# Gates behind the last mixer head, rho by Ln and Exp, and a tail laid out by token halves

## The chip, the cores and the metric

The kernel runs on one core of one Trainium2 chip. The metric is the device time of one execution in microseconds (us). A core has a matrix engine (TensorE, PE in the profile, with its weight loads as PEld), a vector engine (DVE), a scalar engine (ACT), a general engine (POOL), and a queue engine (SP) that here only issues transfers. Each works through its own instructions in order and waits for the others by semaphores. Transfers can be issued from SP and from POOL; sixteen DMA engines carry them out.

## The reference

One layer of a decoder trunk on 528 tokens (16 meta tokens, then 512), width 2048, and a final norm. Cut to what is computed:

```python
u = rmsnorm(h, norm1_g)                       # h: 528 x 2048
v_pool, v_lru, v_gelu, g_pool, g_lru = split(u @ w_in)
pool_out = per_group((window_mean(v_pool) - v_pool) @ pool_w) * pool_scale
xc = causal_conv4(v_lru)
r, i = sigmoid(xc @ gate_a + ab), sigmoid(xc @ gate_x + xb)   # per head of 256
a = exp(-8 * r * softplus(-lam))
state[t] = a[t] * state[t-1] + sqrt(1 - a**2)[t] * (i * xc)[t]
lru_out = state * gelu(v_gelu)
merged = sigmoid(g_pool) * pool_out + sigmoid(g_lru) * lru_out
h = h + merged @ w_out
h = h + relu(rmsnorm(h, norm2_g) @ w1)**2 @ w2
out = rmsnorm(h, final_g)[16:]
```

Channels lie on partitions, tokens in the free dimension.

## The kernel before

Every product is a sum of three: both operands are split into a rounded part (hi) and the rest (lo), and hi x hi, hi x lo and lo x hi add up in one PSUM bank. A class of its own, W (L45 to L161), brings the weights in chunks of 128 x 1024: SP issues the loads (L103), DVE adds raw chunks where a block form needs sums of them (L124), ACT makes the hi part (`whi`, L132), DVE the lo part (`wlo`, L133). Four raw buffers and four hi and lo buffers rotate; W.advance() prepares up to two splits ahead of the one in use, W.ready(n) goes on to split n.

The program runs through these stages.

1. Mixers, to about 480 us of the profile: a list of jobs written out by hand (L255 to L257). VL makes a channel block of the recurrence's input, VP one of the pooling input with its window sums on POOL (L542), GA the gates of a head (PE L363 into `ga`, sigmoids L496, and then the whole LRU: exponentials L506 to L508, the Sqrt L515, DVE steps, and a scan L524 whose result goes to DRAM, L525), PW the linear map of a pooling group (PE L358 into `ps_pw`, ACT copies `po` L564, a transfer L565). The list ends with VP_15, GA_7, PW_3.
2. Gates, from about 480 us: eight blocks each of three column ranges of w_in (gl, ge, gp), each block by seven products in place of eight (x11, t1, t2, ... of Strassen's kind; function strassen, L622). gl0 is the first. Its first product in bank A is copied by ACT to p1 (L642), another to u2 (L664), one of bank B to q5 (L646); DVE adds the banks to these (L742).
3. w_out with the residual, the row sums of squares and the second norm. finish_h (L809) writes a pair of row blocks of h to DRAM; middle (L948) is run after the first block of w1's products and makes rho, a factor per token, from PE's sum over partitions `ps_r`.
4. w1 with squared ReLU in 32 blocks, spilled to DRAM, and 5. w2 in groups, added into h by accumulating transfers.
6. The tail (L1103 to L1178): the last contributions to h for 16 row blocks m, first for token half 0, then for half 1; each is added into `acc` (L1157), squared (L1160), and the squares are added on POOL (L1164). norm_out (L1111) sums them over partitions on PE (L1114), and makes the factor r by Ln and Exp with one correcting step on DVE (L1117 to L1124); scale_out (L1130) applies it and issues the output's transfers on SP (L1139).

The order on each engine is set by a scheduler in the framework that places instructions by estimated costs when they become ready, within the order that data, buffers and explicit ties demand: `tc.issue_after(x)` places what is issued in it behind x, and a manual dependency does the same for a pair. One such tie, W.behind, is set in the last head's LRU: it holds DVE's weight sums of the first gates' splits that are prepared after that behind the last scan. Buffers of one name rotate; where a pool closes, the next pool in the same place waits for what still uses it.

## Time and profile before

| what | us |
|---|---|
| median of three runs (lowest, highest) | 2408.87 (2406.92, 2414.11) |
| the profiled execution | 2410.42 |
| its span, first to last instruction | 2408.6 |
| PE busy in it | 2362.7 |
| DVE busy | 1926.1 |
| ACT busy | 1211.2 |
| POOL busy | 310.0 |

The span is the core's time from the first to the last instruction; 1.8 us lie around it. Times in the rows are counted from its start. Busy shares are averages over stages with different limits, so the stages of the change are read on PE's timeline. A row of a timeline has the start, the length, the engine, the line, the operation with its output and inputs, and in brackets how long the engine stood idle before it and what ended that. An `x8` means that eight like instructions in a row are put in one.

### The profile page before, as it was taken

The page shows a single profiled execution, that of the slowest core. Times are in us where ns is not written, and L with a number is a line of the kernel's source. Part 1 is how long each engine was busy: PE and PEld are TensorE (multiplying, and loading weights), DVE is VectorE, ACT ScalarE, POOL GpSimd, SP SyncE. Part 2 cuts the span into 40 slices and gives each one's busy share as a digit, 9 for nine tenths or more (in the row PEclk, how much of TensorE's full clock was granted, in tenths as well). Part 3 has the DMA queues.
Part 4 walks back from the last instruction along what each step waited for, and adds up shares of the span by engine and source line. Part 5 has one row for each costly group of instructions (what it writes and reads, how often), then busy time and mean ns, then how long its engine had stood idle before and what let it go on. Part 6 is the DMA issues. An engine that isn't in the chain of part 4 may idle for free. (4 is left out here: it accounts for less than half of the span.)

```text
span 2408.6 us, 46240 instructions
## 1 busy us (share of the span) xinstructions
PE 2362.7 (98%) x19252; PEld 2313.6 (96%) x19252; DVE 1926.1 (80%) x2359; ACT 1211.2 (50%) x1631; POOL 310.0 (13%) x428
## 2 busy tenths in 40 slices
PE   8999999999999999999999999999989999999997
PEld 8999999999999999888999999999989999999997
DVE  7867766578888886378989888888879888888877
ACT  6654554445555554244445444444455555555544
POOL 0224343300000000022000000000100000000013
PEclk9999999999999999999999999999989999999998
DMA  5255555744444447568544545544576666666653
GB/s 196 88 167 175 173 169 183 259 171 141 149 141 149 157 151 266 166 214 279 163 156 152 160 152 164 166 161 156 186 202 172 178 179 193 187 189 184 169 183 105
DMA packets 119890, 418.73 MB, mean 174 GB/s; under 512 B 13888, under 2 KB 25280, under 8 KB 118016
## 3 DMA queue, kind: packets, MB, share of 16 engines
q1 hardware_dynamic: 78224, 251.82, 32.8%
q0 software_dynamic: 41312, 163.86, 21.3%
q8 instruction: 150, 2.46, 0.4%
q14 instruction: 60, 0.49, 0.1%
q10 hardware_dynamic: 144, 0.10, 0.0%
HBM read 324.89 MB, written 90.31 MB: 172 GB/s over the span
## 5 line engine op out<-in xcount | busy, mean ns | idle before, releaser
L133 DVE TENSOR_TENSOR wlo<-raw,whi 128x1024 fp32r<-128x1024 f32 (+2 forms) x388 | 467.6, 1207 | 127.4 <-ACT whi L132 127.1
L132 ACT ACTIVATE whi<-raw 128x1024 fp32r<-128x1024 f32 (+2 forms) x388 | 399.2, 1034 | 336.7 <-issue 88.1
L132 ACT ACTIVATE whi<-sum 128x1024 fp32r<-128x1024 f32 (+3 forms) x267 | 278.9, 1044 | 465.3 <-DVE sum L124 240.7
L133 DVE TENSOR_TENSOR wlo<-sum,whi 128x1024 fp32r<-128x1024 f32 (+3 forms) x267 | 320.7, 1201 | 80.7 <-ACT whi L132 76.4
L363 PE MATMUL ps_A<-a,whi 128*128 128x256 f32 x2048 | 359.0, 279 | 1.8 <-ACT whi L132 1.6
L363 PE MATMUL ps_Ab<-a,whi 128*128 128x256 f32 x1728 | 310.9, 280 | 3.5 <-DVE a L1002 1.7
L363 PEld LDWEIGHTS ps_A<-a,whi 128*128 128x128 f32 x2048 | 311.1, 189 | 2.9 <-ACT whi L132 1.8
L363 PE MATMUL ps_A<-a,wlo 128*128 128x256 f32 x1024 | 285.0, 278 | 0.0
L363 PEld LDWEIGHTS ps_Ab<-a,whi 128*128 128x128 f32 x1728 | 264.7, 190 | 4.1 <-DVE a L1002 1.9
L363 PE MATMUL ps_Ab<-a,wlo 128*128 128x256 f32 x864 | 242.0, 280 | 0.0
L124 DVE TENSOR_TENSOR sum<-sum,raw 128x1024 f32<-128x1024 f32 (+4 forms) x178 | 213.7, 1201 | 5.4
L363 PEld LDWEIGHTS ps_A<-a,wlo 128*128 128x128 f32 x1024 | 193.4, 189 | 0.0
L363 PE MATMUL ps_B<-a,whi 128*128 128x256 f32 x1024 | 177.8, 277 | 0.0
L363 PEld LDWEIGHTS ps_Ab<-a,wlo 128*128 128x128 f32 x864 | 164.6, 190 | 0.0
L363 PE MATMUL ps_vl<-a,whi 128*128 128x272 f32 (+1 forms) x896 | 163.3, 285 | 0.0
L363 PE MATMUL ps_vp<-a,whi 128*128 128x256 f32 (+1 forms) x896 | 162.8, 284 | 0.0
L363 PE MATMUL ps_wo<-a,whi 128*128 128x512 f32 x512 | 158.3, 390 | 0.0
L363 PEld LDWEIGHTS ps_B<-a,whi 128*128 128x128 f32 x1024 | 154.3, 188 | 0.1
L363 PE MATMUL ps_Bb<-a,whi 128*128 128x256 f32 x864 | 153.8, 278 | 0.0
L363 PE MATMUL ps_B<-a,wlo 128*128 128x256 f32 x512 | 141.9, 277 | 0.8 <-DVE wlo L133 0.8
L124 DVE TENSOR_TENSOR sum<-w,raw 128x1024 f32<-128x1024 f32 (+3 forms) x89 | 106.5, 1197 | 41.9 <-DMA raw<-w 37.8
L363 PEld LDWEIGHTS ps_vl<-a,whi 128*128 128x128 f32 x896 | 138.3, 189 | 0.3
(330 smaller groups left out, 5863.4 us busy)
## 6 DMA issues: line engine op xcount, KB each, us to landing
raw<-w SPq DMA_DIRECT2D x168, 512.0 KB, 4.3
raw<-w_in SPq DMA_DIRECT2D x135, 512.0 KB, 3.7
w<-w SPq DMA_DIRECT2D x56, 512.0 KB, 4.2
a<-ysp POOLq DMA_DIRECT2D x27, 896.0 KB, 6.3
hsp<-e POOLq DMA_DIRECT2D x33, 512.0 KB, 6.0
ysp<-t POOLq DMA_DIRECT2D x31, 512.0 KB, 5.0
w<-w_in SPq DMA_DIRECT2D x24, 512.0 KB, 3.8
ysp<-y POOLq DMA_DIRECT2D x31, 384.0 KB, 5.1
```

The lines of the kernel that those rows point to most:

```text
L124: nc.vector.tensor_tensor(self.raw[o], self.raw[x], self.raw[y], op=ALU.add)
L132: nc.scalar.activation(hi[:, s], raw[:, s], AF.Copy)
L133: nc.vector.tensor_tensor(lo[:, s], raw[:, s], hi[:, s].bitcast(F32), op=ALU.subtract)
L363: PE.matmul(o, a, b, start=first and i == 0, stop=last and i == 2, skip_group_check=True)
```

## The change

It has three parts and some moves that go with them.

**Mixers to gates.** The last head's sigmoids are no longer behind the first weight splits of the gates: W.hold ties the first one (whi80) behind the last sigmoid. The LRU of that head becomes a function of its own that is run behind PW_3, with W.ready to the second and fourth split of the first block before and between. The last group's pooling results get buffers from the ring in which the inputs of the recurrence are kept (`keep`, four buffers, two of them still held by the last head's), and their transfers and the last head's go on SP's queue instead of POOL's. For gl0, p1 and u2 lie in the buffer `scale`, which is not in use then, instead of the blocks' own pool; a manual tie puts the copy to p1 behind the first Sqrt, and the advance of the weights behind that copy.

**Rho.** pre_scale also makes v2 = s2 * s2 / D and loads the table of Ln and Exp, a load that stood at the tail. In middle, rho comes from Ln and Exp with one correcting step, in place of Sqrt, RECIPROCAL and one correcting step.

**Tail.** `acc` is laid out by pair, token half and row block, so that an output transfer has 2 KB in a row on each side instead of twice 1 KB, with the output tensor shaped to match and put in order on the host. The first norm's sums on PE come behind m = 3 of the second half and its factor behind m = 5 (both were behind m = 2). In the second half one square fewer is added on POOL; it goes to PE alone. finish_h writes h in the new layout, two transfers for one, and put_plain's results for w2 are laid out in the same way.

```diff
@@ Weights._split
-            nc.scalar.activation(hi[:, s], raw[:, s], AF.Copy)
+            with self.hold(i) if self.hold else contextlib.nullcontext():
+                nc.scalar.activation(hi[:, s], raw[:, s], AF.Copy)
@@ before the jobs
+        for i in range(2):
+            keep(f"turn{i}")
@@ job_GA
-                    S.activation(s, tokens(t), AF.Sigmoid,
+                    opened = S.activation(s, tokens(t), AF.Sigmoid,
...
+            if hd == HEADS - 1:
+                W.hold = lambda i: (tc.issue_after(opened.ins) if i == W.first_set
+                                    else contextlib.nullcontext())
+                W.ready(W.first_set + 2)
             W.advance()
+            if hd == HEADS - 1:
+                rest.append(lambda: lru(hd, pt))
+            else:
+                lru(hd, pt)
+        def lru(hd, pt):
...
-                S.activation(r, r, AF.Sqrt)
+                root = S.activation(r, r, AF.Sqrt)
+                if hd == HEADS - 1 and co == 0:
+                    W.root = root
...
-                G.dma_start(lr_sp[c % 8][:, c // 8, :], x[:, META:])
+                queue = nc.sync if hd == HEADS - 1 else G
+                queue.dma_start(lr_sp[c % 8][:, c // 8, :], x[:, META:])
@@ job_PW
-                z = tmp(f"po{c}")[:, :SEQ]
+                z = (keep if g == 3 else tmp)(f"po{c}")[:, :SEQ]
                 S.activation(z, t, AF.Copy, scale=pv("ps", c))
-                G.dma_start(pl_sp[c % 8][:, c // 8, :], z)
+                queue = nc.sync if g == 3 else G
+                queue.dma_start(pl_sp[c % 8][:, c // 8, :], z)
+            if rest:
+                W.ready(W.first_set + 4)
+                rest.pop()()
@@ strassen
+        if name == "gl0":
+            p1, u2 = scale[:, :HS], scale[:, HS:SEQ]
...
-                S.activation(p1, A, AF.Copy)
+                done = S.activation(p1, A, AF.Copy)
+                if name == "gl0":
+                    tc.add_manual_dep(W.root.ins, done.ins.name, ...
...
-                after(r)
-                W.advance()
+                done = after(r)
+                with tc.issue_after(done.ins) if name == "gl0" and r == "x11" else contextlib.nullcontext():
+                    W.advance()
@@ put_plain
-        n = 2 * int(c[0]) + int(c[1]) - 3
+        n = a + 2 * b if by_half else 2 * a + b
@@ finish_h
-        G.dma_start(h_sp[p].rearrange("p (a s) -> p a s", a=2), h)
+        for b in range(2):
+            dst = h_sp[p][:, b * SEQ : (b + 1) * SEQ].rearrange("p (a s) -> p a s", a=2)
+            G.dma_start(dst, h[:, :, b * HS : (b + 1) * HS])
@@ pre_scale
         S.activation(v2, s2, AF.Sqrt)
+        tc.keep_in_program_order(S.preload_act_table_set("natural_log_exp_and_others"))
         V.reciprocal(s2, v2)
+        V.scalar_tensor_tensor(v2, s2, 1.0 / D, s2, op0=ALU.mult, op1=ALU.mult)
@@ middle
+        V.scalar_tensor_tensor(rho, t, EPS * D, v2, op0=ALU.add, op1=ALU.mult)
...
-            V.tensor_scalar(a, t, 1.0 / D, EPS, op0=ALU.mult, op1=ALU.add)
-            for _ in range(2):
-                V.tensor_tensor(a, a, s2, op=ALU.mult)
-            S.activation(b, a, AF.Sqrt)
-            V.reciprocal(rho, b)
-            V.tensor_tensor(b, rho, rho, op=ALU.mult)
-            V.scalar_tensor_tensor(b, b, -0.5, a, op0=ALU.mult, op1=ALU.mult)
-            V.scalar_tensor_tensor(rho, b, 1.5, rho, op0=ALU.add, op1=ALU.mult)
+            S.activation(b, rho, AF.Ln)
+            S.activation(a, b, AF.Exp, scale=-0.5)
+            V.tensor_tensor(b, a, a, op=ALU.mult)
+            V.scalar_tensor_tensor(b, b, -0.5, rho, op0=ALU.mult, op1=ALU.mult)
+            V.scalar_tensor_tensor(rho, b, 1.5, a, op0=ALU.add, op1=ALU.mult)
@@ tail
-            ht = hp.tile([P, KD, SEQ], F32, name="acc")
+            ht = hp.tile([P, KD // 2, 2, 2, HS], F32, name="acc")
...
-    def norm_out(i, xs):
+    def total(i, xs):
         t = ps.tile([P, 512], F32, tag="ps", name=f"ps_n3_{i}")[:, :HS]
         for k, x in enumerate(xs):
             PE.matmul(t, ones, x, start=k == 0, stop=k == len(xs) - 1, skip_group_check=True)
+        return t
+
+    def root(i, t):
...
-            dst = out_d[m - 1 : m + 1, :, i * HS : (i + 1) * HS].rearrange("m p s -> p m s")
-            nc.sync.dma_start(dst, ht[:, m - 1 : m + 1, c])
-
-    tc.keep_in_program_order(S.preload_act_table_set("natural_log_exp_and_others"))
+            nc.sync.dma_start(out_d[m // 2, i], ht[:, m // 2, i].rearrange("p a s -> p (a s)"))
...
-            elif m < KD - 2:
+            elif m < KD - 2 - i:
                 G.tensor_tensor(sums[m % 2], sums[m % 2], q, op=ALU.add)
...
-            if i == 1 and m == 2:
-                r = norm_out(0, pend)
+            if i == 1 and m == 3:
+                pend = total(0, pend)
+            if i == 1 and m == 5:
+                r = root(0, pend)
...
-    r = norm_out(1, pend)
+    r = root(1, total(1, pend))
```

What moves on the engines stands in the order of their instructions (line, operation, output and inputs with buffer numbers; `whi80` is the hi part of weight split 80, the first of gl0, `gs700` the first sigmoid of the last head, `ga700` its bank, `a2` the input of the last pooling product, `po12` to `po15` the last group's results). First ACT from the mixers to the gates, before:

```order
L132 ACTIVATE whi79_5404<-raw79_5151 128x1024
L132 ACTIVATE whi80_5465<-raw80_5205 128x1024
L132 ACTIVATE whi81_5513<-sum80_5511 128x1024
L496 ACT_TABLE_LOAD
L496 ACTIVATE gs700_5357<-ga700_5344,par_71 128x528
L548 ACTIVATE a2_897<-pd15_5333 128x512
...
L564 ACTIVATE po12_5449<-ps_pw12_5436,par_71 128x512
...
L564 ACTIVATE po14_5495<-ps_pw14_5482,par_71 128x512
...
L132 ACTIVATE whi82_5569<-sum80_5511 128x1024
L132 ACTIVATE whi83_5598<-raw83_5473 128x1024
...
L642 ACTIVATE p1_gl0_5540<-ps_Agl0_5537 128x256
...
L664 ACTIVATE u2_gl0_5541<-ps_Agl0_5537 128x256
```

And in the change, where `scale_80` with 256 columns is first p1, then u2:

```order
L134 ACTIVATE whi79_5406<-raw79_5153 128x1024
L500 ACT_TABLE_LOAD
L500 ACTIVATE gs700_5359<-ga700_5346,par_71 128x528
L565 ACTIVATE a2_899<-pd15_5335 128x512
...
L134 ACTIVATE whi80_5410<-raw80_5207 128x1024
L134 ACTIVATE whi81_5420<-sum80_5418 128x1024
...
L581 ACTIVATE po14_5475<-ps_pw14_5462,par_71 128x512
...
L134 ACTIVATE whi83_5499<-raw83_5424 128x1024
...
L529 ACT_TABLE_LOAD
...
L667 ACTIVATE scale_80<-ps_Agl0_5548 128x256
...
L134 ACTIVATE whi84_5628<-w2181_5414 128x1024
...
L695 ACTIVATE scale_80<-ps_Agl0_5548 128x256
```

The sigmoids stand ahead of whi80, po14 and whi83 ahead of the last Sqrt, p1 behind it, and whi84 to whi87, which stood ahead of p1 or u2, behind p1. On SP's queue in the same place, where before nothing stood between the loads:

```order
L104 DMA w2185_5428<-w_in 128x1024
L583 DMA pl4_167<-po12_5443 128x512
...
L583 DMA pl7_170<-po15_5491 128x512
L542 DMA lr7_162<-xc15_5212 128x512
L104 DMA raw86_5632<-w_in 128x1024
L104 DMA raw87_5664<-w_in 128x1024
```

Four pl transfers and lr7, the last channel's, stand ahead of the loads raw86 and raw87.

Then DVE at rho (`scale_80` is s2 and later rho; `r2a` and `r2b` are work buffers), before:

```order
L958 TENSOR_SCALAR r2a_12532<-ps_r_12522 128x512
...
L960 TENSOR_TENSOR r2a_12532<-r2a_12532,scale_80 128x512
...
L960 TENSOR_TENSOR r2a_12532<-r2a_12532,scale_80 128x512
...
L962 RECIPROCAL scale_80<-r2b_12533 128x512
...
L963 TENSOR_TENSOR r2b_12533<-scale_80 128x512
...
L964 SCALAR_TENSOR_TENSOR r2b_12533<-r2b_12533,r2a_12532 128x512
L133 TENSOR_TENSOR wlo291_12581<-raw216_12243,whi291_12580 128x1024
L965 SCALAR_TENSOR_TENSOR scale_80<-r2b_12533,scale_80 128x512
L124 TENSOR_TENSOR sum216_12609<-w21217_12245,raw218_12464 128x1024
```

and in the change:

```order
L989 SCALAR_TENSOR_TENSOR scale_80<-ps_r_12532,v2_11055 128x512
L135 TENSOR_TENSOR wlo289_12503<-sum212_12348,whi289_12502 128x1024
...
L997 TENSOR_TENSOR r2b_12544<-r2a_12543 128x512
...
L998 SCALAR_TENSOR_TENSOR r2b_12544<-r2b_12544,scale_80 128x512
L135 TENSOR_TENSOR wlo291_12589<-raw216_12251,whi291_12588 128x1024
L999 SCALAR_TENSOR_TENSOR scale_80<-r2b_12544,r2a_12543 128x512
...
L125 TENSOR_TENSOR sum216_12617<-w21217_12253,raw218_12474 128x1024
```

Three of the steps and the RECIPROCAL are gone, and the weight sums and the lo parts of splits move up by as much.

Last DVE in the tail, where half 1 goes on and the first norm's factor `r3_0` is made, before:

```order
L1157 TENSOR_TENSOR acc_26763<-ps_w2l_1_2_27354,acc_26763 128x256
L1119 TENSOR_SCALAR r3_0_27370<-ps_n3_0_27365 128x256
...
L1124 SCALAR_TENSOR_TENSOR ps_r3_0_27376<-r3_0_27370 128x256
L1136 SCALAR_TENSOR_TENSOR acc_26763<-acc_26763,par_71,ps_r3_0_27376 128x256
L1157 TENSOR_TENSOR acc_26763<-ps_w2l_1_3_27378,acc_26763 128x256
L1136 SCALAR_TENSOR_TENSOR acc_26763<-acc_26763,par_71,ps_r3_0_27376 128x256
L1157 TENSOR_TENSOR acc_26763<-ps_w2l_1_4_27389,acc_26763 128x256
```

and in the change:

```order
L1191 TENSOR_TENSOR acc_26771<-ps_w2l_1_3_27372,acc_26771 128x256
L1156 TENSOR_SCALAR r3_0_27412<-ps_n3_0_27383 128x256
L1191 TENSOR_TENSOR acc_26771<-ps_w2l_1_4_27388,acc_26771 128x256
...
L1161 SCALAR_TENSOR_TENSOR ps_r3_0_27418<-r3_0_27412 128x256
L1172 SCALAR_TENSOR_TENSOR acc_26771<-acc_26771,par_71,ps_r3_0_27418 128x256
L1191 TENSOR_TENSOR acc_26771<-ps_w2l_1_6_27420,acc_26771 128x256
L1172 SCALAR_TENSOR_TENSOR acc_26771<-acc_26771,par_71,ps_r3_0_27418 128x256
```

The factor's steps stand between the additions into `acc` (L1157 before, L1191 in the change) instead of in one row, three row blocks later.

More of the change, by code (lines that the diff above doesn't have):

```diff
@@ L59, in __init__ @@
         self.behind = lambda i: contextlib.nullcontext()
+        self.hold = None
     def chunk(self, src):
@@ L641, in after @@
             if r == "x11":
-                S.activation(p1, A, AF.Copy)
+                done = S.activation(p1, A, AF.Copy)
+                if name == "gl0":
+                    tc.add_manual_dep(W.root.ins, done.ins.name,
+                                      mybir.DependencyInfo(mybir.DependencyClass.NoSync, mybir.DependencyReason.DATA),
+                                      reason="order")
+                return done
             elif r == "x21":
@@ L692, in strassen_pair @@
         A, B, C = ([bank(x, name) for name in names] for x in "ABC")
-        puts = [put_plain(e) for e in es]
+        puts = [put_plain(e, True) for e in es]
         spare = {"p1": scale[:, :HS], "u2": scale[:, HS:SEQ], "q5": es[1][:, 3 * HS :]}
@@ L1155, in build @@
                 W.advance()
-            h = ht[:, m, c]
+            h = ht[:, m // 2, i, m % 2]
             V.tensor_tensor(h, t, h, op=ALU.add)
@@ L1221 @@
     h = np.empty((KD, P, SEQ), np.float32)
-    for i in range(KD):
-        h[ORDER[i // 2] + 8 * (i % 2)] = got[i]
+    for q in range(KD // 2):
+        for a in range(2):
+            for b in range(2):
+                h[ORDER[q] + 8 * a, :, b * HS : (b + 1) * HS] = got[q, b, :, a * HS : (a + 1) * HS]
     return c(h.reshape(D, SEQ).T).reshape(1, SEQ, D)
```

19 lines of the change are left out of this document (11 added, 8 removed).

## The prediction

> **What bounds the kernel now.** I read the page first: engines, then the slices of the clock.
>
> ```profile
> span 2408.6 us, 46240 instructions
> PE 2362.7 (98%) x19252; PEld 2313.6 (96%) x19252; DVE 1926.1 (80%) x2359; ACT 1211.2 (50%) x1631; POOL 310.0 (13%) x428
> PEclk9999999999999999999999999999989999999998
> ```
>
> TensorE (PE) is busy 98% at nearly full clock, and no part of the change removes a matmul; so it can only win idle time, half clock, and the end behind the last product. The waits of PE, with sum, count and longest, say where idle time is:
>
> ```profile
> PE ps_Agl L363 <- ACT p_gl L642: 3.5, 1, 3.5
> PE ps_pw L358 <- ACT gs L496: 3.1, 1, 3.1
> ```
>
> Both, the largest that the change touches, lie in the passage from mixers to gates. Then I read PE's timeline at these places and at the end (start, length, instruction, idle before with what ended it).
>
> **Part 1, mixers to gates.** PE's rows are the first pooling product, the first and the resuming gl0 product, and gl0's last; then three stretches (length, busy time of PE, PEld, DVE, ACT, POOL, clock, DMA share, GB/s).
>
> ```profile
> 466.75 0.73 PE L358 MATMUL ps_pw<-a,whi 128*128 128x512 f32 x2 [3.09 <-ACT gs L496]
> 479.60 0.40 PE L363 MATMUL ps_Agl<-a,whi 128*128 128x256 f32 x2
> 486.94 0.39 PE L363 MATMUL ps_Cgl<-a,wlo 128*128 128x256 f32 x1 [0.95 <-DVE wlo L133]
> 493.30 0.80 PE L363 MATMUL ps_Agl<-a,whi 128*128 128x256 f32 x2 [3.49 <-ACT p_gl L642]
> 507.08 0.28 PE L363 MATMUL ps_Agl<-a,wlo 128*128 128x256 f32 x1
> ...
> 468.20:471.60 3.40, 3.40 (x10) 2.68 (x9) 0.35 (x1) 3.37 (x6) 2.51 (x2) 0.55 1.00 396
> 493.20:498.60 5.40, 5.30 (x25) 5.30 (x26) 4.92 (x5) 0.33 (x2) 0.54 (x1) 0.50 0.81 310
> 498.60:502.00 3.40, 3.40 (x29) 3.25 (x29) 1.23 (x1) 1.33 (x2) 0.00 (x0) 1.00 0.49 154
> ```
>
> The last stretch prices a 256-column matmul at full clock: 3.40 / 29 = 0.117. The pooling products (48 of 512 columns, twice that each by estimate) are 11.3, gl0 (7 x 24) 19.7, together 31.0. From 463.66 (466.75 less 3.09) to 507.36 are 43.7 us, so 12.7 are lost: 7.5 idle (3.09 + 0.95 + 3.49), the rest nearly all half clock, one window of 3.4 us behind each long idle time, some 1.7 us each, with the second longer.
>
> ACT around the first idle time, ACT's copy that ends the second, and DVE's last scan:
>
> ```profile
> 463.63 1.06 ACT L132 ACTIVATE whi<-sum 128x1024 fp32r<-128x1024 f32 x1 [4.80 <-PE ga L363]
> 464.70 1.28 ACT L496 ACT_TABLE_LOAD   x1
> 466.00 0.70 ACT L496 ACTIVATE gs<-ga,par 128x528 f32<-128x528 f32 x1
> 467.19 0.63 ACT L548 ACTIVATE a<-pd 128x512 fp32r<-128x512 f32 x1 [0.49 <-DVE pd L545]
> 492.87 0.38 ACT L642 ACTIVATE p_gl<-ps_Agl 128x256 f32<-128x256 f32 x1 [1.61 <-DMA lr<-xc]
> 481.02 1.26 DVE L524 TENSOR_TENSOR_SCAN xc<-n,gs 128x528 f32<-128x528 f32 x1
> ```
>
> The weight split stood, waiting 4.80 us, ahead of the sigmoid for which the pooling product's bank waits; the change puts the sigmoids first. So 3.09 goes. What is late next is the last pooled block: its hi split is at 467.19 behind a DVE result whose POOL sums do not move by more than a microsecond, and the products reach it earlier than now. I take back 1.5. The window then holds less idle than today's, its half clock goes too (+1.7): 3.09 - 1.5 + 1.7 = 3.3, and gl0 starts near 476.3.
>
> gl0 today takes 27.8 us for 19.7 of work, so 8.1 lost. The copy at 492.87 waited for the buffer of a result's transfer; in the change p1 and u2 lie in another place and this wait is gone. New is that ACT reaches p1 only behind the Sqrt, and that behind the fourth block result, po14, whose buffer po12's transfer must have left. That transfer, now on SP's queue, is issued near 473 while the DMA engines are full. Its price is the row of a weight load in such a time:
>
> ```profile
> raw<-w_in SPq DMA_DIRECT2D x1, 512.0 KB, 10.7
> 454.00:456.00 2.00, 2.00 (x19) 2.00 (x18) 1.43 (x2) 0.00 (x0) 0.00 (x0) 1.00 1.10 459
> ```
>
> The transfer is half as large and today's rush ends near 480, so it lands at 477 to 480. From there the rows behind it on ACT (po14 0.69, e1 0.63, whi83 1.06, po15 0.69, load 1.28, Sqrt 0.70) put p1's start between PE's need, 476.3 + 48 x 0.117 = 481.9, and 484.8: idle 0 to 2.9. Behind p1 stand the splits that today come before it: whi84 and its lo part, among the last head's DVE steps; the third product waits 2.3 to 3.2 for them. With no or two half-clock windows (0 to 3.4) gl0 loses 3.1 to 8.5: against 8.1 a gain of 5.0 to a loss of 0.4, and with the 3.3 the whole is 2.9 to 8.3. I take 5: nearer the low end, since ACT and DVE are in order here and nothing of the last head's work has gone. On SP the loads raw86 and raw87 now stand behind four pl transfers and lr7, which waits for the last scan (482.3 today); at 0.33 an issue that costs nothing while the scan ends before some 490.
>
> The Trainium skill, "DMA: Bandwidth & Descriptors", section "Queues, rings and completion order", says that a DMA engine takes packets from its queues in turn. By that the small transfer would not wait for the fills ahead of it, p1 would be at 482 and the gain 8. The 10.7 us of a load issued amid such fills speak against it.
>
> **Part 2, rho.** PE first, then DVE, with ACT's root:
>
> ```profile
> 1134.67 1.13 PE L952 MATMUL ps_r<-ssq,ones 128*128 128x512 f32 x2 [2.42 <-DVE ssq L820]
> 1144.89 0.50 PE L363 MATMUL ps_A<-a,whi 128*128 128x256 f32 x2 [0.21 <-DVE y L1025]
> 1151.72 0.39 PE L363 MATMUL ps_B<-a,wlo 128*128 128x256 f32 x1 [0.76 <-DVE wlo L133]
> 1156.16 0.51 PE L363 MATMUL ps_A<-a,whi 128*128 128x256 f32 x2 [1.57 <-ACT whi L132]
> 1157.11 0.62 PE L363 MATMUL ps_C<-a,whi 128*128 128x256 f32 x2 [0.44 <-ACT whi L132]
> ...
> 1136.80 0.69 DVE L958 TENSOR_SCALAR r2a<-ps_r 128x512 f32<-128x512 f32 x1
> 1141.21 3.35 DVE L962 RECIPROCAL scale<-r2b 128x512 f32<-128x512 f32 x1
> 1147.41 0.69 DVE L965 SCALAR_TENSOR_TENSOR scale<-r2b,scale 128x512 f32<-128x512 f32 x1
> 1148.01 1.22 DVE L124 TENSOR_TENSOR sum<-w,raw 128x1024 f32<-128x1024 f32 x1
> ...
> 1157.70:1161.10 3.40, 3.40 (x19) 3.40 (x19) 3.40 (x4) 0.30 (x1) 0.32 (x1) 0.55 0.56 189
> ```
>
> DVE runs without a gap here, and the four stalls behind ps_r (0.21, 0.76, 1.57, 0.44, together 2.98) are splits that come late because of it; the half clock behind them costs 1.7 more. Before, rho takes the TENSOR_SCALAR, two products, the 3.35 RECIPROCAL and three more: six of some 0.69 and one of 3.35, 7.5 us. After, four of 0.69, 2.8. ACT does Ln and Exp where it did one Sqrt, 0.63 more on an engine half idle. So DVE reaches the sum of 1148.01 some 4.7 us sooner, more than any of the stalls sums to, and the splits are in time: 2.98 + 1.7 = 4.7, less a remainder of 0.2: 4.5. The 2.42 stay. Bounds: if these 2.42 alone now bring a half-clock window, 1.7 less; with all other small gaps gone 5.8.
>
> The Trainium skill, "TensorE: Matmul & The Clock Gate", section "HAM oscillation — how this bites in real kernels", asks for idle gaps beyond some 3.4 us before the clock falls. By that no stall of 1.57 would cost half clock. The 0.55 behind 1157.70 says that it does, and I go by the row.
>
> The table of Ln and Exp is loaded earlier, in ACT's idle time of the w_out stage, and one v2 operation is added to DVE there:
>
> ```profile
> 1031.10 1.06 ACT L132 ACTIVATE whi<-raw 128x1024 fp32r<-128x1024 f32 x1 [2.77 <-PE ps_wo L363]
> 1116.34 0.59 POOL L812 DMA_DIRECT2D hsp<-h  x1 [5.91 <-DVE h L811]
> ```
>
> 2.77 of idle hold a load of 1.28; uncovered it would cost that. The eight added h_sp transfers are eight issues of 0.59 on a POOL that waits 5.91 before one; I take nothing, at most 0.6 if the last is late.
>
> **Part 3, the tail.** The first and the second norm's sums on PE, and POOL, ACT, DVE around the second:
>
> ```profile
> 2378.78 2.25 PE L1114 MATMUL ps_n<-sqo,ones 128*128 128x256 f32 x8 [0.23 <-POOL sqo L1164]
> 2392.10 3.49 PE L1114 MATMUL ps_n<-sqo,ones 128*128 128x256 f32 x8 [1.89 <-POOL sqo L1164]
> 2384.82 7.92 POOL L1164 TENSOR_TENSOR sqo<-sqo,sqo 128x256 f32<-128x256 f32 x11 [4.50 <-ACT sqo L1160]
> 2395.63 0.47 ACT L1117 ACTIVATE r<-ps_n,eps 128x256 f32<-128x256 f32 x1 [3.39 <-PE ps_n L1114]
> 2391.64 2.43 DVE L1136 SCALAR_TENSOR_TENSOR acc<-acc,par,ps_r 128x256 f32<-128x256 f32 x6
> 2396.13 0.42 DVE L1119 TENSOR_SCALAR r<-ps_n 128x256 f32<-128x256 f32 x1 [2.06 <-ACT r L1117]
> ...
> 2402.00:2403.00 1.00, 0.00 (x0) 0.00 (x0) 0.18 (x1) 0.00 (x0) 0.48 (x1) 0.50 1.02 339
> ```
>
> POOL, 0.72 an addition, ends the second norm's sums late; with one fewer it is done 0.7 earlier and PE starts the sums near 2390.8, before the last square (2391.7). The ten rows that replace eight are 10 x 0.281 = 2.8 at full clock (2.25 / 8 each), so Ln is at 2393.5 instead of 2395.63. By then DVE, with one scaling more left over, is free at 2394.1: its chain starts 2.0 before 2396.13. At half clock (3.49 / 8 = 0.436 each) the ten take 4.4 and 0.5 is left. All that follows moves with it, and the outputs, 2.1 MB at 339 GB/s for some 6.2 us, go in 2 KB instead of 1 KB pieces: nothing, or at 459 GB/s (the row above) 1.6 less; I take 0.6, nearer to nothing since the scalings feed them. Together 2.6 (0.5 to 3.6). Splitting the first norm costs nothing while DVE waits for no result of it.
>
> **Sum.** 5 + 4.5 + 2.6 = 12.1. The profiled execution took 2410.42 around its span of 2408.6, so 2398.3 by that; it stands 1.55 above the median of the runs shown, 2408.87. By the median: 2396.8, so 2397.
>
> **Rivals.** *The small transfer doesn't wait* (the rule of queues in turn, 0.15): ACT's po14 and so p1 are free in time, part 1 gives 8: 2394. Against it the 10.7. *The passage gives nothing* (0.2): ACT and DVE keep all the last head's steps, and put behind the first splits they stall gl0 as the copy did, 8.5 lost and no half clock saved ahead: 2402. For it: 31.0 us of work in which DVE and ACT are nearly as busy. *Given back later* (0.12): half-clock windows follow the phase at which a stall falls in a window of 3.4 us; later stalls move by some 10 us and one or two more windows, 1.7 each, join, or part 2's 2.42 bring one: 2402 to 2406. *Slower* (0.06): SP is in order, and the weight loads behind lr7 wait for the last scan; if the scan, now behind the first splits, ends after 496, four loads (2.1 MB) land at over 510 where one landed at 493 today, gl0 and the next gates wait up to 14 more, with half clock 17 to 20: 2414 to 2418. Against it: only some 4 us of DVE work are put ahead of a scan that ends at 482.3. The first splits' hold acting on nothing is excluded by the order of ACT.
>
> **How the numbers follow.** Forecast 0.47, own range 2391 to 2402; with the rivals, 2388 to 2408 holds over 8 in 10. What a measurement can tell here is 0.3%, 7.2 us: faster means below 2401.6, slower above 2416.1. Faster: forecast and small transfer 0.62, and half of the two rivals near 2402 less their upper part, 0.1: 0.72; same 0.22; slower 0.06.
>
> **What would show it.** Right: no idle ahead of the first pooling product, gl0's end 3 to 8 earlier against its ga; no stall over 0.5 from 1140 to 1160 and clock 1.00 there; Ln of the second norm 2 earlier against the last product. Wrong: po14 or p1 waiting beyond 485, splits behind the scans, or a raw load landing after the product that wants it; a clock near 0.55 behind the 2.42; half clock in the second norm; new half-clock windows later.

## The result

| kernel | median of its runs, us | lowest to highest | runs |
|---|---|---|---|
| before | 2410.09 | 2406.92 to 2414.11 | 4 |
| changed | 2396.22 | 2394.30 to 2398.78 | 4 |

The ratio of the changed kernel to the one before is 0.9948, 95% interval 0.9935 to 0.9962. By the time before that is some 12.5 us less, between 9 and 16; 12.1 had been worked out. The profiled execution of the changed kernel has a span of 2396.2, where 2408.6 stood before. In the experiments below, one execution each of rho alone (6087 us), of the whole change (3935) and of the kernel before (3943) was far slower than all others and is left out of every median and ratio.

**From mixers to gates, after.** PE's timeline from the last gate product to gl0's last matmul, with the idle times in between (start, length, instruction, idle before):

```profile
466.21 0.28 PE L365 MATMUL ga<-xs,wlo 128*128 128x256 f32 x1
466.33 0.63 PE L360 MATMUL ps_pw<-a,whi 128*128 128x512 f32 x2
469.35 0.50 PE L360 MATMUL ps_pw<-a,whi 128*128 128x512 f32 x1 [0.76 <-ACT a L565]
482.31 0.50 PE L365 MATMUL ps_Bgl<-a,whi 128*128 128x256 f32 x2 [0.36 <-ACT po L581]
487.04 0.50 PE L365 MATMUL ps_Agl<-a,whi 128*128 128x256 f32 x2 [1.72 <-ACT scale L667]
495.22 0.50 PE L365 MATMUL ps_Agl<-a,whi 128*128 128x256 f32 x2 [2.26 <-ACT scale L695]
505.65 0.28 PE L365 MATMUL ps_Agl<-a,wlo 128*128 128x256 f32 x1
```

The 3.09 of idle ahead of the first pooling product is gone: the product starts as the gate product ends. What was expected next has come, 0.76 for the last pooled block, and then 1.72 for p1 and 2.26 for u2. From 466.49 to 505.93 are 39.4 us, where it was 43.7. On ACT, po14 waits for the transfer as the prediction had it, and p1 stands behind it:

```profile
481.57 0.69 ACT L581 ACTIVATE po<-ps_pw,par 128x512 f32<-128x512 f32 x1 [1.25 <-DMA pl<-po]
486.62 0.37 ACT L667 ACTIVATE scale<-ps_Agl 128x256 f32<-128x256 f32 x1
491.68 1.06 ACT L134 ACTIVATE whi<-w 128x1024 fp32r<-128x1024 f32 x1 [4.16 <-DVE w L125]
```

**Rho, after.** PE's one wait there:

```profile
1134.16 2.07 PE L988 MATMUL ps_r<-ssq,ones 128*128 128x512 f32 x2 [3.35 <-DVE ssq L854]
```

and two stretches (length, busy time of PE, PEld, DVE, ACT, POOL with the number of instructions, clock, DMA share, GB/s):

```profile
1133.90:1137.30 3.40, 3.14 (x8) 2.11 (x9) 3.40 (x5) 2.03 (x3) 0.00 (x0) 0.50 0.64 212
1138.00:1163.00 25.00, 25.00 (x220) 25.00 (x220) 24.29 (x34) 11.96 (x15) 1.64 (x3) 1.00 0.58 192
```

Behind 1138 there is no idle time left and no half clock: 220 matmuls in 25 us. The like stretch of the kernel before held 166:

```profile
1140.00:1165.00 25.00, 22.03 (x166) 21.12 (x166) 22.84 (x29) 9.38 (x12) 1.61 (x3) 0.93 0.38 122
```

54 more at 0.117 are 6.3 us. But ahead of them there is now a half-clock window that the profile before had not in this place, and the wait for the last row sum is 3.35 instead of 2.42.

**The tail, after.** PE's sums for the second norm, ACT's Ln and DVE's first step of the factor:

```profile
2381.80 2.42 PE L1148 MATMUL ps_n<-sqo,ones 128*128 128x256 f32 x10 [1.21 <-POOL sqo L1198]
2384.26 0.47 ACT L1154 ACTIVATE r<-ps_n,eps 128x256 f32<-128x256 f32 x1 [1.49 <-PE ps_n L1148]
2384.91 0.43 DVE L1156 TENSOR_SCALAR r<-ps_n 128x256 f32<-128x256 f32 x1
```

and a stretch in which the last outputs leave:

```profile
2390.00:2391.00 1.00, 0.00 (x0) 0.00 (x0) 0.84 (x3) 0.00 (x0) 1.00 (x2) 0.50 1.03 383
```

Ten sums at full clock take 2.42, where eight at half clock took 3.49. The last product ends at 2380.59 (2390.22 before), so Ln comes 3.67 behind it instead of 5.41, the span's end 15.6 instead of 18.4, 2.8 less. The outputs leave at 383 GB/s instead of 339; 2.1 MB take 0.7 less by that.

Laid side by side, matmul by matmul, the two traces differ so: up to the last gate product the changed kernel is 2.8 behind; the passage gives 4.3; up to the sum for rho 0.9 is lost; rho's stage gives 4.9, its new half-clock window counted against it; from there to the last product 4.2 more; the tail 2.8. The sum is 12.5. Two of these terms, the first and the one of 4.2, lie where the order of PE is as it was. The first w2 groups hold most of the second:

```profile
1745.00:1810.00 65.00, 56.24 (x414) 54.17 (x412) 48.49 (x68) 36.01 (x61) 5.90 (x8) 0.89 0.70 204
```

```profile
1738.00:1801.00 63.00, 54.99 (x423) 52.58 (x423) 48.76 (x68) 35.53 (x61) 6.67 (x10) 0.95 0.73 220
```

The first row is before, the second after: more matmuls in 2 us less, at a clock of 0.95 instead of 0.89. The stalls are nearly the same ones; the half clock behind them is not. Whether the change does that, or chance, is the first question for the experiments.

### The profile page after: what moved, and what is told of

The parts are those of the page before. It is cut to its first block, busy times and chain, and to the rows that moved or that the text cites. A ratio compares the mean times of both kernels' runs of the same rounds, so it can differ in the third digit from the quotient of the medians.

```text
span 2396.2 us, 46247 instructions
## 1 busy us (share of the span) xinstructions
PE 2355.8 (98%) x19254; PEld 2307.7 (96%) x19254; DVE 1921.9 (80%) x2357; ACT 1212.7 (51%) x1632; POOL 313.1 (13%) x429
## 5 line engine op out<-in xcount | busy, mean ns | idle before, releaser
L365 PEld LDWEIGHTS ps_vp<-a,whi 128*128 128x128 f32 x896 | 138.2, 188 | 0.0
```

What stands on the lines that cost most here:

```text
L365: PE.matmul(o, a, b, start=first and i == 0, stop=last and i == 2, skip_group_check=True)
```

## The experiments

Each kernel was timed together with the kernel before, on one chip. Ratios are to before, with 95% intervals; one thousandth is 2.4 us.

| run | ratio | interval | median, us |
|---|---|---|---|
| passage alone | 0.9985 | 0.9976 to 0.9993 | 2404.96 |
| rho alone | 0.9974 | 0.9964 to 0.9984 | 2402.47 |
| tail alone | 0.9992 | 0.9983 to 1.0001 | 2405.70 |
| the whole change again | 0.9954 | 0.9940 to 0.9967 | 2396.35 |
| whole, sum for rho asked for later | 0.9951 | 0.9937 to 0.9964 | 2397.68 |
| hold alone | 0.9987 | 0.9977 to 0.9997 | 2404.50 |
| p1 and u2 alone | 0.9987 | 0.9978 to 0.9996 | 2406.39 |
| whole, transfers on POOL's queue | 0.9955 | 0.9942 to 0.9969 | 2398.85 |
| whole, t2's split ahead of the forms | 0.9948 | 0.9935 to 0.9960 | 2395.33 |
| whole without rho | 0.9976 | 0.9967 to 0.9985 | 2402.98 |
| whole, five splits ahead of the LRU | 0.9950 | 0.9936 to 0.9964 | 2396.57 |
| hold, rho and tail | 0.9960 | 0.9946 to 0.9975 | 2397.09 |

**The three parts alone, and the whole.** My theory: each part pays where it acts, and they add. The rival: a good part of the gain is half-clock windows that fell out by phase.

The passage alone has the hunks of the change from W.hold to the strassen function, and nothing else.

> Only the passage from mixers to gates is changed (hold, LRU behind the last pooling group, own buffers, SP queue, p1 and u2 elsewhere); rho and tail stay as before. Theory A (each part pays where it acts): 4 to 5 us less than before, ratio 0.9980, with gl0 ended 39 to 40 us after the last gate product instead of 43.7. Theory B (a good third of the whole gain is not this part's or any part's, but half-clock windows that fell out by phase in the first w2 groups): the same 4 to 5 here at gl0's end, but not more than 3 left at the end of the span over many runs, because windows come back later. Theory C (the wait goes behind the first splits): within 1 us of before.

Rho alone:

```diff
+        tc.keep_in_program_order(S.preload_act_table_set("natural_log_exp_and_others"))
+        V.scalar_tensor_tensor(v2, s2, 1.0 / D, s2, op0=ALU.mult, op1=ALU.mult)
...
+            S.activation(b, rho, AF.Ln)
+            S.activation(a, b, AF.Exp, scale=-0.5)
```

> Only rho by Ln and Exp (with v2 and the earlier table load); passage and tail as before. Theory A: 4.5 us less than before, ratio 0.9981; no stall over 0.5 between 1140 and 1160, PE waits 2.4 for the row sums. Theory B: the stalls go, but the wait for the row sums is 3.3 and brings a half-clock window there, so 3 us less, ratio 0.9988.

The tail alone has the layout, finish_h, put_plain, total and root, and the square that POOL no longer adds.

> Only the tail (layout by token halves with 2 KB transfers, two h_sp transfers for one, first norm's sums and factor later, one square less on POOL); passage and rho as before. Theory A: 2.6 us less than before, ratio 0.9989, span's end 15.6 us behind the last product instead of 18.4. Theory B: the eight added h_sp transfers make the weight loads before the row sums late, PE waits 3.3 there instead of 2.4, and 1.7 are left, ratio 0.9993.

> The changed kernel once more, beside its three parts. Theory A: 12 us less than before, ratio 0.9950, and equal to the sum of the three parts within 1.5 us. Theory B (phase): the sum of the parts falls 3 to 4 us short of it or the whole comes out at 9 us.

By the ratios the passage gives 3.6 us, rho 6.3, the tail 1.9, together 11.8; the whole, timed beside them, gives 11.1. So they add, as theory A has it, as far as intervals of 2 us to each side of a part, and 3 of the whole, can tell. Of the expectations for the parts, the passage's (theory A 4 to 5, theory B not more than 3) stay undecided by time, and so do the tail's (2.6 or 1.7). Rho's interval, 3.9 to 8.7, holds theory A's 4.5 and not theory B's 3, though theory B's sign came: PE waits 2.52 for the row sums there, with a half-clock window behind.

The profile of the tail alone shows what the 4.2 between rho and the last product were. In this kernel neither the passage nor rho is changed, and its first w2 groups read

```profile
1743.00:1807.00 64.00, 55.56 (x425) 53.00 (x424) 48.64 (x69) 36.02 (x61) 6.25 (x9) 0.95 0.72 216
```

as the changed kernel's do: clock 0.95, not the 0.89 of the profile before. And the changed kernel itself, profiled a second time in the run called the whole change again, has the 0.89:

```profile
1737.00:1800.00 63.00, 53.81 (x395) 51.79 (x395) 45.39 (x65) 33.48 (x57) 6.10 (x9) 0.89 0.70 209
```

So this term is not the change's. The one profiled execution of before happened to have more half clock than any of the thirteen others: 13.7 us lost by it between 60 us and 2370, against 5.1 to 11.9. A run's mean clock goes with its time only loosely: over the 25 runs of the kernel before that stand beside these four kernels, the six at 0.992 have a median of 2410.6, the five at 0.993 one of 2410.4, the eleven at 0.994 one of 2406.7 and the three at 0.995 one of 2408.3. The 2.8 lost ahead of the passage are not the change's either. PE's clock is full from 14.4 us on instead of 10.5, and the kernel is 1.6 behind from there; a wait of 1.4 near 255 adds the rest, and it stands in twelve of the fourteen profiles, also in that of rho alone, whose mixers are those of before:

```profile
253.79 0.73 PE L358 MATMUL ps_pw<-a,whi 128*128 128x512 f32 x2 [1.62 <-DVE v L470]
```

So two profiles are not to be subtracted over their whole length; the stage has to be read.

How much of rho's gain its own stage shows is seen with the half-clock window on both sides. The tail-alone kernel, with the old rho, has in this stage

```profile
1135.80:1139.20 3.40, 3.40 (x18) 3.40 (x17) 2.96 (x4) 1.83 (x2) 0.00 (x0) 0.50 0.71 167
1140.00:1165.00 25.00, 22.12 (x185) 21.27 (x183) 23.90 (x29) 10.91 (x14) 1.64 (x3) 1.00 0.37 125
```

and on PE's timeline

```profile
1134.51 0.70 PE L955 MATMUL ps_r<-ssq,ones 128*128 128x512 f32 x1 [2.29 <-DVE ssq L823]
1156.82 0.50 PE L363 MATMUL ps_A<-a,whi 128*128 128x256 f32 x2 [1.58 <-ACT whi L132]
```

The same stalls as before, 1.58 among them, but no half clock behind them, and the window behind the wait for the row sum, as after the change. 185 matmuls against the 220 of the changed kernel: 35 at 0.117 are 4.1 us. With the window behind the stalls it is 6.3. That window belongs to the phase, not to the change: the same stalls of 1.58 and 0.45 bring it in one execution and not in another. All profiles together say the same. Over the same 470 products around the sum for rho, the six kernels with the old rho take 66.1 to 68.1 us, the seven with the new one and this order 62.2 to 64.6; the medians, 66.8 and 63.0, are 3.8 apart.

**Rho taken out of the whole.** The changed kernel with middle and pre_scale as before and the table load at the tail:

> The changed kernel with rho by Sqrt and RECIPROCAL as before: passage and tail only. Theory A (rho is worth what its stalls are in the traces, 3 for the stalls and 1 to 1.5 for half clock and a remainder): 4 to 4.5 us slower than the changed kernel, ratio to before 0.9972. Theory B (rho is worth 6 as it measured alone): ratio 0.9980.

0.9976, halfway between the two expectations. Against the changed kernel's 0.9948 and 0.9954 that makes rho worth 5 to 7 us, as alone (6.3). The traces show 4.1 without the window and 6.3 with it. The intervals are 4 us wide and hold both, so whether more than the stage's own 3.8 is won stays open; no trace shows where the rest would lie.

**What carries the passage.** Two of its moves were tried alone on the kernel before, and the whole was reduced to the first of them. The hold alone:

```diff
+            with self.hold(i) if self.hold else contextlib.nullcontext():
+                nc.scalar.activation(hi[:, s], raw[:, s], AF.Copy)
...
+            if hd == HEADS - 1:
+                W.hold = lambda i: (tc.issue_after(opened.ins) if i == W.first_set
+                                    else contextlib.nullcontext())
```

> Before, with only the tie of the first split (whi80) behind the last sigmoid; LRU, buffers and queues as before. Theory A (the order of the sigmoids is what the pooling products waited for, the moved LRU is needed so that gl0 doesn't pay for it): no idle of 3.1 ahead of the first pooling product, but whi80 and whi81 now stand behind the LRU on ACT and gl0's first product waits for them 2 to 4 us; together 0 to 2 us worse than before. Theory B (the sigmoids alone carry the gain): 3 us less than before.

p1 and u2 alone:

```diff
+        if name == "gl0":
+            p1, u2 = scale[:, :HS], scale[:, HS:SEQ]
```

> Before, with only p1 and u2 of gl0 in another place. Theory A (the transfer of the last scan is what the copy to p1 waited for): the idle of 3.5 ahead of t2 goes or is under 1, with a half-clock window: 3 to 5 us less than before, as much as the whole passage. Theory B (the copy is late because ACT's splits stand ahead of it, the transfer only comes last): under 2 us less.

The hold follows theory B: 3.1 us less (0.7 to 5.5), as much as the whole passage (3.6) within the intervals. Its rows:

```profile
479.01 0.50 PE L365 MATMUL ps_Agl<-a,whi 128*128 128x256 f32 x2 [0.93 <-ACT whi L134]
482.53 0.58 PE L365 MATMUL ps_Agl<-a,wlo 128*128 128x256 f32 x1 [3.02 <-DVE wlo L135]
503.55 0.28 PE L365 MATMUL ps_Agl<-a,wlo 128*128 128x256 f32 x1
```

and the whole stage, from the last gate product to gl0's end:

```profile
465.36:503.83 38.47, 33.53 (x218) 30.11 (x218) 27.27 (x31) 22.06 (x30) 9.84 (x14) 0.96 0.98 327
```

The wait that theory A expected is there, 0.93 and 3.02, because the first splits now stand behind the LRU. But the later wait of 3.49 for p1 is gone, without any move of p1, and the stage takes 38.5 us, against 39.4 in the changed kernel and 43.7 before. ACT's copy to p1 still waits for the buffer that the last scan's transfer leaves, only sooner. POOL's issues before, with the first of them the last 2 MB fill:

```profile
481.48 0.55 POOL L229 DMA_DIRECT2D a<-fsp_t  x1
482.57 0.55 POOL L525 DMA_DIRECT2D lr<-xc  x1 [0.54 <-DVE xc L524]
```

and in the hold alone, with ACT's copy:

```profile
483.94 0.54 POOL L530 DMA_DIRECT2D lr<-xc  x1 [1.47 <-DVE xc L529]
484.47 0.55 POOL L231 DMA_DIRECT2D a<-fsp_t  x1
...
487.19 0.38 ACT L647 ACTIVATE p_gl<-ps_Agl 128x256 f32<-128x256 f32 x1 [5.56 <-DMA lr<-xc]
```

Before, the small transfer is issued behind the fill in the same queue, and the copy that waits for it stands 10.3 us behind its issue (492.87). Here it is issued ahead of the fill, and the copy stands 3.2 behind. The profile before has the like in itself: the other transfer of this kind, issued at 480.95, just ahead of the fill, lands 2.9 later. That this order is what shortens it is read from the rows; no run changed the order of these two issues alone.

p1 and u2 alone give 3.1 too (1.0 to 5.3), the low end of theory A's 3 to 5; theory B's under 2 lies in the interval. There the 3.49 shrinks to 0.55, and 0.73 and 1.21 come up behind it:

```profile
488.94 0.50 PE L363 MATMUL ps_Agl<-a,whi 128*128 128x256 f32 x2 [0.55 <-ACT scale L646]
498.73 0.39 PE L363 MATMUL ps_Bgl<-a,wlo 128*128 128x256 f32 x1 [0.73 <-DVE wlo L133]
502.80 0.51 PE L363 MATMUL ps_Agl<-a,whi 128*128 128x256 f32 x2 [1.21 <-DVE zgl L750]
```

So each of two moves gives about 3, and both with the moved LRU, the buffers and the queue give 3.6, each known to 2 us or so. The whole change with nothing of the passage but the hold says the same:

> The changed kernel with the passage cut down to the tie of the first split behind the last sigmoid: the LRU in its old place, buffers, queues, p1 and u2 as before; rho and tail as changed. Theory A (of the passage only the sigmoids' order carries the gain, as the hold alone and the whole passage each measured 3 to 4 us): ratio to before 0.995, as the changed kernel. Theory B (the other moves carry something too): 1.5 to 3 us slower than the changed kernel, ratio 0.9963.

0.9960 with 0.9946 to 0.9975, median 2397.09. Neither theory falls: the changed kernel measured 0.9948 and 0.9954, with medians of 2396.22 and 2396.35.

The stage's length in all profiles tells more. The two other kernels that have this stage as before, rho alone and the tail alone, take 41.0 and 41.3 for it, not 43.7, with the same waits (7.6 and 7.8 of idle, 7.5 before). The difference is half clock behind the wait for p1. Rho alone has that wait, and behind it no half clock:

```profile
494.73 0.50 PE L363 MATMUL ps_Agl<-a,whi 128*128 128x256 f32 x2 [3.22 <-ACT p_gl L642]
496.50:499.90 3.40, 3.38 (x29) 3.17 (x28) 3.40 (x5) 1.33 (x2) 0.00 (x0) 1.00 0.77 288
```

With the passage of the change the stage takes 38.2 to 39.8 in six profiles (38.3 in the passage alone, for 39 to 40 expected), and 38.5 with the hold alone. Divided at gl0's first product, the pooling part goes from 15.9 to 12.6 in all six (13.7 with the hold alone), but gl0 itself takes 25.6 to 27.3, against 25.0 and 25.4 in the two kernels named. So the passage wins its time in the pooling part, by the order of the sigmoids, and gl0 wins nothing by the other moves together. With p1 and u2 alone, and the LRU in its old place, gl0 takes 23.0; the hold together with that was not run.

**The queue.** `queue = G` at both places, the order on ACT row for row as in the changed kernel:

> The changed kernel with the last results' transfers on POOL's queue again; the order on ACT is the same, row for row. Theory A (po14 waits for po12's transfer wherever it is issued; the queue decides when it lands): on POOL's queue, behind fills of 2 MB, it lands up to 5 us later, p1 with it: 2 to 5 us slower than the changed kernel, about 2400. Theory B (queues are served in turn or the DMA engines are shared anyway): within 1 us of the changed kernel.

0.9955, nearer to theory B, though the median, 2398.85, is 2.5 above the changed kernel's, and the intervals of 3 us to each side hold both theories. Theory A was right on the wait: po14 waits longer, and the stage feels it at another product (ACT, then PE):

```profile
481.20 0.69 ACT L581 ACTIVATE po<-ps_pw,par 128x512 f32<-128x512 f32 x1 [3.00 <-DMA pl<-po]
```

```profile
481.94 0.50 PE L365 MATMUL ps_Bgl<-a,whi 128*128 128x256 f32 x2 [2.14 <-ACT po L581]
486.22 0.50 PE L365 MATMUL ps_Agl<-a,whi 128*128 128x256 f32 x2 [1.29 <-ACT scale L667]
```

2.14 ahead of B and 1.29 ahead of t2, where it was 0.36 and 1.72: 1.4 more, and the stage is 40.4 long for 39.4. Five runs don't tell 1.4 from nothing.

**Five splits ahead of the LRU.** `W.ready(W.first_set + 5)` in the whole:

> The changed kernel with five instead of four splits of gl0 made ahead of the last head's LRU. Theory A (the waits of 1.7 to 2.4 for u2 and 2.3 for p1 are splits and LRU steps that change places; whi84 ahead of p1 moves the wait from u2 to p1): within 1 us of the changed kernel, p1 about 1 later and u2 about 1 to 2 sooner. Theory B (u2's wait for DVE is what costs): 2 to 3 less, with a half-clock window gone.

0.9950, theory A. The wait for u2 is gone, and the one for p1 is 4.24:

```profile
488.36 0.80 PE L365 MATMUL ps_Agl<-a,whi 128*128 128x256 f32 x2 [4.24 <-ACT scale L667]
```

1.72 and 2.26, together 3.98, in the changed kernel, 4.24 here. In all versions of the passage, from the last gate product to gl0's end, 4.5 to 6.9 us stay idle and only change their place.

**The wait for the row sums.** After rho's stalls went, PE's wait of 2.3 to 3.4 ahead of the sum for rho, and the half-clock window behind it, are the largest loss left in the stage. A first kernel asked for the sum behind the x22 product:

> The changed kernel, and the row sums for rho (PE) one product later: behind x22 of the first w1 block instead of behind t3, with the copies that need rho behind them. Theory A: PE's wait for the last row sum, 2.3 to 3.4 in every profile so far, and the half-clock window behind it are idle time that a product of 2.8 fills, and rho comes no later, so 4 to 5 us less than the changed kernel, about 2392. Theory B: rho then comes a product later, the results that need it hold the banks, and the gain is given back within the first two blocks: within 1 us of the changed kernel, about 2397.

0.9951, as the changed kernel, but it tested nothing: the scheduler left PE's order as it was, product for product, and the wait stands.

```profile
1131.84 2.07 PE L990 MATMUL ps_r<-ssq,ones 128*128 128x512 f32 x2 [2.61 <-DVE ssq L856]
```

What keeps t2 from filling the wait is on DVE: t2's lo part is made between the last two row sums. So a second kernel has that split made ahead of the last pair's forms:

```diff
+            W.ready(W.used + 1)
             head()
```

> The changed kernel, and the weight split of the first w1 block's fourth product (t2) made ahead of the last pair's forms on DVE, not between the two last row sums of squares; the scheduler then puts PE's sum for rho behind t2 by itself. (The kernel that asked for the sum later left it where it was on PE.) Theory A (PE's idle 2.4 to 3.4 there is t2's lo part standing 1132.3 to 1133.5 on DVE, and the half-clock window that follows is its price): the idle is under 1.2, no half clock behind it, and 3 to 4 us less than the changed kernel, about 2393. Theory B (DVE is the bound of the whole stage, its work only changes places): the idle comes back at the next products, within 1 us of the changed kernel.

The mechanism holds in part. The sum for rho stands behind t2 and waits for nothing, and no half clock follows; but 1.83 of idle are left, ahead of t2, where theory A had under 1.2:

```profile
1129.50 0.50 PE L365 MATMUL ps_A<-a,whi 128*128 128x256 f32 x2 [1.83 <-ACT p L667]
```

and the stretches around and behind it:

```profile
1129.00:1140.00 11.00, 10.40 (x81) 9.62 (x82) 11.00 (x15) 6.17 (x10) 0.00 (x0) 1.00 0.71 231
1140.00:1163.00 23.00, 23.00 (x205) 23.00 (x204) 22.65 (x31) 10.76 (x13) 1.65 (x3) 1.00 0.53 192
```

Over the same 470 products the stage takes 60.9 instead of 63.0, 2.0 less, for 3 to 4 expected. In time it is not settled: five runs have a median of 2395.33, ratio 0.9948, beside the changed kernel's 2396.22 and 2396.35. It is the lowest median of all, by less than the runs can tell.

## Why the prediction was right, and where it was not

*The sum.* 2397 was predicted and 2396.22 came. Its three terms were 5, 4.5 and 2.6. Alone they measured 3.6 (1.7 to 5.8), 6.3 (3.9 to 8.7) and 1.9 (nothing to 4.1), and each term lies in its interval. That the sum met the time to within 1 us is partly luck: by the runs of the parts the first term was 1.4 too high, the second 1.8 too low and the third 0.7 too high, and these cancel. The stages themselves, over all profiles, give some 3 for the passage (41.3 to 38.4 by the medians), 3.8 for rho and 2.8 for the tail (18.4 to 15.6). That is some 9.5 of the 11 to 12.5 measured; where the rest lies no trace shows.

*The passage.* Right: the 3.09 went with its half-clock window, and gl0 starts 3.4 sooner behind the last gate product, for 3.3 in the prediction. The pooled block came late instead (0.76 and 0.23 for the 1.5 taken back), po14 waited for its transfer and p1 for po14, and the idle ahead of t2 and t3 is 1.72 and 2.26, for 0 to 2.9 and 2.3 to 3.2. po12's transfer took 5.9 us (475.63 to 481.49); the bounds had 4 to 7.

Wrong is the rest of the term, 1.7 from gl0. The prediction took the 8.1 that gl0 loses in the profile before as the price of its waits, and of that 3.4 were two half-clock windows that the same waits don't bring in rho alone or the tail alone. gl0 lost 7.2 in the changed kernel's profile, but against those two it is no shorter at all: the wait for p1's buffer is gone, and waits for po14, for p1 behind it and for splits stand in its place. Moving p1 alone does shorten gl0 by 2.0 to 2.4; with the other moves that is gone again. And the hold alone removes the 3.49 as well, since the transfer then lands sooner. So the sum counted a second gain where one idle time was only exchanged for others, and the whole passage is worth little more than the hold. Two sums there are also off: the rows behind po12's transfer make 5.05, so p1 starts by 485.1 and not 484.8; and the terms of gl0's loss, 0 to 2.9, 2.3 to 3.2 and 0 to 3.4, make 2.3 to 9.5 and not 3.1 to 8.5.

*The rule of queues in turn* had a rival of its own (2394, 0.15). Its condition did not come: po14 did wait 1.25 for the small transfer. On SP's queue, with fills of 0.8 to 2 MB from POOL's queue under way beside them, the four transfers of 256 KB took 5.9, 5.6, 8.0 and 6.2 us; one issued at 489.94, when the engines were a third busy, took 2.0. So a queue of its own did not spare a small transfer the wait here; in what turns the engines served the two queues no run tells.

*Rho.* Right: the four stalls went altogether, since DVE reaches the sums that much sooner; the stage gives 3.8 for the 4.5. The bound for a half-clock window behind the wait for the row sum (1.7 less) was needed in this profile, but not as a loss by the change: the passage alone and the tail alone, with the old rho, have that window too. In the kernel before the one behind the stalls stood in its place. The wait itself is 2.3 to 2.8 in the six profiles with the old rho and 2.5 to 3.35 in the seven with the new one, 2.95 in the second of the changed kernel; whether the change adds to it stays open.

*The clock rule.* The Trainium skill, "TensorE: Matmul & The Clock Gate", section "Part 1: The HAM clock gate (the "warmup" mystery)", says that the window of some 3.4 us is free-running and doesn't start with the kernel. The runs bear that out. In the profile before, the half-clock stretches that start at 467.85, 491.74, 1157.34 and 1751.26 lie 7, 202 and 376 windows of 3.413 us behind the first, and from one profile to the next this grid of windows lies differently against the program.

That decides which stalls cost half clock. I count, for each window of the grid at full clock from 60 us to 2370 in the fourteen profiles, the time in which no matmul runs. Behind all 61 windows with 1.88 us or more of it, the next window is at half clock; behind the 9339 with less than 1.77 none is; of the five between, three are. So idle time of a little over half a window is enough, if it falls into one window, and the prediction did right to go by its row. None of the 61 is idle as a whole; 3.28 is the most. The section that the prediction quoted from the Trainium skill, "TensorE: Matmul & The Clock Gate", "HAM oscillation — how this bites in real kernels", asks for gaps beyond some 3.4 us, and the traces don't agree. A wait of 3.45 in the tail alone, longer than a window, costs no half clock, since it is cut into 1.87 and 1.58. The stalls of 1.57 and 0.44 fall into one window in the profile before, of which PE is busy for 1.40, and the next is at half clock:

```profile
1153.90:1157.30 3.40, 1.40 (x9) 0.98 (x9) 2.55 (x4) 2.61 (x4) 0.53 (x1) 1.00 0.51 167
1157.30:1160.70 3.40, 3.40 (x17) 3.40 (x17) 3.40 (x5) 0.70 (x1) 0.00 (x0) 0.51 0.55 206
```

In the tail alone the border between two windows cuts the same stalls in two, and the clock stays full:

```profile
1152.90:1156.30 3.40, 2.34 (x20) 2.14 (x19) 3.05 (x6) 0.96 (x2) 0.61 (x2) 1.00 0.29 116
1156.30:1159.70 3.40, 2.43 (x17) 2.22 (x18) 2.90 (x3) 2.36 (x3) 0.49 (x1) 1.00 0.87 300
```

*The tail.* PE's sums start 1.21 behind the last product for 1.89, at full clock, and take 2.42 for the 2.8 estimated. DVE's chain starts 4.32 behind the last product instead of 5.91, 1.6 sooner for the 2.0; it waits for DVE's own last scalings, as was said. From there to the end 11.3 are left where it was 12.5; the outputs' rate makes 0.7 of that, for 0.6 taken. The nine profiles with the new tail end 15.6 to 16.0 behind the last product, the five with the old one 17.2 to 19.1.

*The rivals.* "The passage gives nothing" falls by the time (interval 1.7 to 5.8), but its mechanism came in part: the last head's steps behind the first splits stall gl0 about as much as the copy did. "Slower" falls, with less to spare than the prediction thought. It put some 4 us of work ahead of a scan that ended at 482.3; the last scan ends at 494.9, which is 9.8 later when the 2.8 ahead of the passage are taken off. The loads raw86 and raw87 were issued from 491.67 all the same, because the transfer ahead of them belongs to the first of the two scans (it leaves at 489.94; the other leaves at 494.94, behind the loads), and no product of gl0 waited for them. "Given back later" is not seen: the first w2 groups have two to four half-clock windows, by the execution, with the change and without it.

## What to carry to other kernels

Where an engine's clock is gated by windows that run on their own, a stall of 2 us costs 2 or 3.7, by where the border of a window falls, and two profiles of one kernel can differ by 3 us (2396.2 and 2399.4 for the changed one here): cost an edit from its stage's stalls, take the half clock behind them from several profiles, and test the edit by parts that are timed many times and must add up. Where a stage has more idle time than any one wait, removing one wait moves the rest; the move that is cheapest to make (here one tie that puts the sigmoids first) may give nearly what all of them give. And a request for another order is only tested when the order of the engine shows it.

## What was not expected

The same stalls, 1.58 and 0.45, brought a half-clock window in one execution and none in another, and a plain count of idle time per window tells which. A wait for a small transfer was not shorter on a queue of its own. Output transfers of 2 KB pieces took the engines from 339 to 383 GB/s in the tail, though the share of the DMA engines' time was full in both. One addition less on POOL (0.72) took the wait ahead of the second norm's sums from 1.89 to 1.21, and the sums ran at full clock, here and in the tail alone (1.19, then ten in 2.43).
